# Two-layer trunk on one core: gate projections moved into their own heads, value tiles behind the next block's projections, boundary transpositions spread

## The chip, the cores and the metric

The kernel runs on one core of a Trainium2 chip. TensorE multiplies matrices, VectorE (DVE), ScalarE (ACT) and GpSimd (POOL) work element by element, and SyncE (SP) issues most transfers (DMAs). The metric is the device time of one execution in microseconds (us); lower is better.

## The reference

Two layers over x of 1 x 1024 x 1024, in fp32; after each a layer norm of alpha * x + layer(x).

```python
def _even_layer(x, ...):
    a_x, a_g, b_q, b_k, b_v, b_g = split(x @ w_in)         # six projections of width 1024
    a_h = _rg_lru(_causal_dwconv(a_x, conv_w, conv_b), ...)  # 8 blocks: gates, then h = a * h + u
    y_a = a_h * silu(a_g)
    # 8 heads: w = exp(log_sigmoid(z) + sum of log_sigmoid(-z) over later keys), strictly causal
    y_b = _stick_breaking(b_q, b_k, b_v) * silu(b_g)
    return concat(y_a, y_b) @ w_out
def _odd_layer(x, ...):
    q, k, v, g = split(x @ w_in)                            # 16 query heads, 2 key/value heads of 64
    o = _swa_sinks_alibi(q, k, v, sinks)                    # window of 128
    return (o * silu(g)) @ w_out
```

## The kernel before

The whole program is one function, `trunk`. Each fp32 operand is kept as a high and a low part, and a product is three matmuls (`mm3`, L110 to L112): high by high, high by low, low by high, mostly on tiles of 128x512. The low part of a result comes from PSUM with a copy on ScalarE and a subtraction on VectorE (`split_psum`, L118 and L119). Weights come in by `load_piece`: a DMA, then two GpSimd operations for the high and the low part (L102, L103). The framework decides the order on each engine from the order of the code, the dependencies and the free buffers.

The work runs in stages. First, eight recurrent blocks: `lru_main(f)` makes the gates of block f, a scan (L492) and a gated output, and stashes it in DRAM. Its own TensorE work is small, so a queue of generators, `Filler` (L34), is pumped between its steps: it takes so much work, by a rate in rough us, and always from the generator that stands first. In the queue are the value tiles (`v_tiles`, table VT: one or two tiles of 8 products x 3 for each block), and the projections of the next block (`lru_proj(f + 1)`: ax and ag, 48 products each). At f == 2 the weights of the second half of the values are loaded (`load_wv(1, d)`): the raw tiles go into buffers of the tags qh and ql, ScalarE casts them (L219), VectorE makes the low part.

Second, eight attention heads (`attn_all`), twelve units each: score z (L313 to L315), mask on the diagonal (L317), two sigmoids (L320, L321), scan (L329), product (L331, B), and, two units later, transpositions of B (L339), eviction (wt), and the products with v (L355 to L362). Between units the filler is pumped with the next head's projections: k, q and g, 48 products each, as `head_proj(n + 1)`. In the last head the filler is `early_out`: 72 products of the output projection into three PSUM tiles (opeX0 to opeX2). They need `prep(0)` to `prep(7)`: two DMAs, casts on ScalarE (L519), a subtraction on VectorE (opwh) and one on GpSimd (opwl), both L521.

Third, the rest of the output projection (`even_products`: the fourth tile opeX3 first, then opeZ; `prep` runs ahead by nine), the loads of x (xpre), and the layer norm, whose scaling runs on GpSimd (L636) and whose last addition runs on VectorE (L641). `x1_transposes(t)` transposes two rows of blocks at a time (L708) into the operands of the next layer. Then the boundary: half 1 of the odd layer's projections ok, ov and oq0, with `x1_transposes(0)` and `(1)` between, then half 0, the attention in windows, and the last output projection.

Of the kernel before, what the change touches and what calls it, by code (L numbers as in the profile page):

```python
# [52 lines left out]
def trunk(ctx, tc, x, xT_in, w_even, w_even_v, w_even_out, w_gate, lru_vec,  # L53
# [113 lines left out]
    def proj_ftile(src, ft, name, evac, halves=(0, 1), eng="pool"):  # L167
        get = w_ftile(src, ft, name, eng)
        for hf in halves:
            yield from proj_half(get, hf, name, evac)  # L170

    ytile = {}
    fill = Filler()
# [18 lines left out]
    def evac_qk(which, n):  # L192
        def f(hf, ps):
            h = wt_(which + "h", f"{which}h{n}_{hf}")
            l = wt_(which + "l", f"{which}l{n}_{hf}")
            split_psum(ps, h, l)
            qk[which, n, hf] = (h, l)
        return f

    def evac_gate(key):  # L200
        def f(hf, ps):
            if hf == 0:
                ytile[key] = slot(f"y{key[0]}{key[1]}", F32)
            y = ytile[key][:, hf, :]
            nc.scalar.activation(y, ps, AF.Sigmoid)
            nc.vector.tensor_tensor(out=y, in0=ps, in1=y, op=ALU.mult)
        return f
# [39 lines left out]
    def head_proj(n):  # L247
        yield from proj_ftile(w_even, 8 + n, f"k{n}", evac_qk("k", n), (1, 0))
        yield from proj_ftile(w_even, n, f"q{n}", evac_qk("q", n), (1, 0))
        yield from proj_ftile(w_even, 16 + n, f"g{n}", evac_gate(("b", n)))  # L250

    def stash(kind, t, tile_):
# [21 lines left out]
    def load_ya(n):  # L274
        ya_in[n] = slot(f"yain{n}", F32)
        for i, kind in enumerate(("A21", "S3")):
            nc.sync.dma_start(ya_in[n][:, i, :], yst[kind, n])
# [16 lines left out]
    rate = [0.0]  # L294

    def attn_all():
# [77 lines left out]
        for idx in range(len(units) + LAG + 1):  # L374
            while vpend:
                v_stage(*vpend.pop(0))
            if idx < len(units):
                n, i, g = units[idx]
                if (i, g) == (NS - 2, 1):
                    w_sums(n)  # L380
                if (i, g) == (NS - 1, 1):
                    fill.drain()
                    load_ya(n)
                    if n + 1 < SB_HEADS:
                        load_v(n + 1)
                        fill.add(head_proj(n + 1))
                        rate[0] = 31.2 / 12
                    else:
                        for t in range(8):
                            prep(t)  # L390
                        fill.add(early_out())
                        rate[0] = 16.4 / 12
                u_stage(n, i, g)
                pend.append(units[idx])
            if idx >= LAG and pend:
                n, i, g = pend.pop(0)
                t_stage(n, i, g)
                if i % 2 == 0 and g == 0:
                    vpend.append((n, i // 2))
            yield  # L400
# [106 lines left out]
    def prep(k):  # L507

        if k >= 8 * len(PRODUCTS):
            return  # L510
        i, t = divmod(k, 8)
        yop, w_op, _ = PRODUCTS[i]
        res = []
        for tag, src in (("wh", yst[yop, t]),
                         ("wl", yst[w_op, t] if isinstance(w_op, str) else w_even_out[w_op[0], w_op[1] + t])):
            raw = wpool.tile([P, HALF], F32, tag=tag, name=f"raw{tag}{k}", bufs=5)
            nc.sync.dma_start(raw, src)
            hl = slot(f"op{tag}{k}", F32R)
            nc.scalar.copy(hl[:, 0, :], raw)  # L519
            eng = nc.vector if tag == "wh" else nc.gpsimd  # L520
            eng.tensor_tensor(out=hl[:, 1, :], in0=raw, in1=hl[:, 0, :].bitcast(F32), op=ALU.subtract)  # L521
            res.append(hl)
        ops[k] = res
# [10 lines left out]
        f(b, y[:, 1, c], w[:, 0, :], start=False, stop=t == 7)  # L534

    def early_out():
        for p in range(3):
            op[0, p] = bank(XB[p], f"opeX{p}")
        for t in range(8):
            for p in range(3):  # L540
                step_mm(t, p)
                yield C_512
# [17 lines left out]
    for f in range(8):  # L560
        q, sts = VT[f]
        if f == 2:
            for d in range(ND):
                load_wv(1, d)
        fill.add(v_tiles(q, sts))
        if f + 1 < 8:
            fill.add(lru_proj(f + 1))
        else:
            load_v(0)
            fill.add(head_proj(0))  # L570
        r = (5.2 * len(sts) + (20.8 if f < 7 else 31.2)) / 4
        for _ in lru_main(f):
            fill.pump(r)
        fill.drain()
# [202 lines left out]
    with ExitStack() as dctx:  # L777
# [176 lines left out]
                pass  # L954

        gk = w_ftile(w_odd, 8, "ok", pool=slots)
        run(proj_half(gk, 1, "ok", evac_k))
        x1_transposes(0)
        xth.update(x1h)
        xtl.update(x1l)  # L960
        gv = w_ftile(w_odd, 9, "ov", pool=slots)
        run(proj_half(gv, 1, "ov", evac_v))
        x1_transposes(1)
        gq = w_ftile(w_odd, 0, "oq0")
        run(proj_half(gq, 1, "oq0", evac_q(0)))
        v_transposes(1)
        run(proj_half(gk, 0, "ok", evac_k))
        run(proj_half(gv, 0, "ov", evac_v))
# [76 lines left out]
```

## Time and profile before

| | |
|---|---|
| time, median of 3 runs | 1261.37 us (1260.93 to 1263.18) |
| the profiled execution's own time | 1261.14 us |
| its span in the profile | 1259.4 us |
| mean granted TensorE clock | 0.994 |
| busy: TensorE / VectorE / ScalarE / GpSimd | 98% / 68% / 50% / 50% |
| HBM traffic | 100.70 MB read, 37.75 MB written |

The span is what the profiler covers; all times of the trace count from its start. Busy shares are means over stages that have different limits. The profiler models the ends of matmuls, which are pipelined, so an end can lie later than the start of the next one. The granted clock is a share of TensorE's full speed.

### The profile page before, as it was taken

How to read it: one execution, taken by the hardware profiler on the slowest of the kernel's cores; microseconds unless marked ns; L12 is line 12 of the kernel's file. 1: busy time of each engine (PE TensorE's matmuls, PEld its weight loads, DVE VectorE, ACT ScalarE, POOL GpSimd, SP SyncE). 2: the span in 40 equal slices, each digit the busy share in tenths (PEclk: the TensorE clock that was granted, in tenths of full speed). 3: DMA queues.
4: the chain of work that ended last, by engine and by line, in shares of the span. 5: the costliest groups of instructions: out<-in, count | busy, mean ns of one | idle time of the engine just before them, and what ended most of it. 6: DMA issues, size and time to landing. Idle time of an engine off the chain costs nothing.

```text
span 1259.4 us, 18456 instructions
## 1 busy us (share of the span) xinstructions
PE 1228.9 (98%) x6176; PEld 1038.1 (82%) x6176; DVE 855.7 (68%) x1705; ACT 623.5 (50%) x1291; POOL 631.1 (50%) x720
## 2 busy tenths in 40 slices
PE   8999999999999999999999899999999999999997
PEld 6888788888888888888887778887888888887886
DVE  7354756556556767667668859587367877788367
ACT  5255546646333434434335447444277777778300
POOL 3334435435625454554445369666455555555440
PEclk9999999999999999999999999999999999999999
DMA  7312422234414254352457299700211101111022
GB/s 256 130 50 76 147 96 80 80 117 143 144 58 150 87 167 134 116 168 74 153 183 227 96 334 313 237 33 27 65 34 35 34 27 34 35 34 60 18 83 101
DMA packets 87791, 139.67 MB, mean 111 GB/s; under 512 B 10000, under 2 KB 27792, under 8 KB 87440
## 3 DMA queue, kind: packets, MB, share of 16 engines
q1 hardware_dynamic: 87696, 138.49, 33.2%
q8 instruction: 49, 0.80, 0.3%
q14 instruction: 46, 0.38, 0.1%
HBM read 100.70 MB, written 37.75 MB: 110 GB/s over the span
## 4 chain that ended last, share of the span: by engine, by line
PE 85%; DVE 6%; DMA 2%; ACT 2%; issue 2%; POOL 2%; POOLq 0%; SPq 0%; DVEq 0%; ACTq 0%
PE pjv L110 2%; PE pjv L111 2%; PE pjv L112 2%; PE pj_k L112 2%; PE pj_k L111 2%; PE pj_q L110 2%; PE pj_k L110 2%; PE pj_oq L110 2%; PE pj_q L112 2%; PE pj_oq L111 2%; PE pj_q L111 2%; PE pj_oq L112 2%; PE pj_og L110 2%; PE pj_g L110 2%; PE pj_og L111 2%; PE pj_g L112 2%
## 5 line engine op out<-in xcount | busy, mean ns | idle before, releaser
L521 POOL TENSOR_TENSOR opwl<-rawwl,opwl 128x512 fp32r<-128x512 f32 x56 | 88.8, 1611 | 36.1 <-ACT opwl L519 35.9
L320 ACT ACTIVATE C<-z 128x512 f32<-128x512 f32 (+3 forms) x96 | 47.4, 494 | 112.8 <-DVE z L317 85.5
L889 POOL TENSOR_SCALAR S<-S,sm 128x256 f32<-128x256 f32 (+1 forms) x128 | 59.8, 482 | 73.0 <-DVE sm L887 28.7
L884 ACT ACTIVATE S<-S,sm 128x256 f32<-128x256 f32 (+1 forms) x128 | 62.5, 490 | 53.6 <-DVE sm L880 51.9
L521 DVE TENSOR_TENSOR opwh<-rawwh,opwh 128x512 fp32r<-128x512 f32 x56 | 72.4, 1326 | 20.2 <-ACT opwh L519 20.1
L331 DVE TENSOR_TENSOR B<-B,C 128x512 f32<-128x512 f32 (+3 forms) x96 | 72.2, 752 | 10.1 <-DVE C L329 0.5
L329 DVE TENSOR_TENSOR_SCAN C<-C,one 128x512 f32<-128x512 f32 (+1 forms) x64 | 60.7, 949 | 16.7 <-ACT C L320 16.6
L118 ACT CAST wt<-tr 128x512 fp32r<-128x512 f32 (+3 forms) x96 | 46.6, 486 | 27.9 <-PE tr L339 27.4
L119 DVE TENSOR_TENSOR wt<-tr,wt 128x512 fp32r<-128x512 f32 (+3 forms) x96 | 52.5, 547 | 7.2 <-ACT wt L118 6.9
L110 PE MATMUL pjv<-wv,xh 128*128 128x512 f32 x128 | 49.9, 401 | 7.7 <-ACT wv L219 7.7
L329 DVE TENSOR_TENSOR_SCAN C<-C,C,one 128x512 f32<-128x512 f32 x32 | 42.0, 1313 | 18.3 <-ACT C L320 18.2
L519 ACT CAST opwh<-rawwh 128x512 fp32r<-128x512 f32 x56 | 34.8, 621 | 36.9 <-DMA rawwh<-stS 15.5
L110 PE MATMUL pj_k<-xh,wh_k 128*128 128x512 f32 x128 | 52.3, 408 | 0.0
L532 PE MATMUL opeX<-opwl,opwh 128*128 128x512 f32 x128 | 51.0, 402 | 1.0 <-DVE pvt L367 1.0
L110 PE MATMUL pj_q<-xh,wh_q 128*128 128x512 f32 x128 | 51.9, 405 | 0.0
L110 PE MATMUL pj_og<-x1h,wh_og 128*128 128x512 f32 x128 | 51.9, 405 | 0.0
L110 PE MATMUL pj_g<-xh,wh_g 128*128 128x512 f32 x128 | 51.8, 405 | 0.0
L110 PE MATMUL pj_oq<-x1h,wh_oq 128*128 128x512 f32 x128 | 51.8, 404 | 0.0
L112 PE MATMUL pj_k<-xh,wl_k 128*128 128x512 f32 x128 | 51.7, 404 | 0.0
L534 PE MATMUL opeX<-opwl,opwh 128*128 128x512 f32 x128 | 51.5, 403 | 0.0
L533 PE MATMUL opeX<-opwl,opwh 128*128 128x512 f32 x128 | 51.5, 403 | 0.0
L339 PE MATMUL tr<-ident,B 128*128 128x128 f32 x288 | 47.3, 273 | 4.2 <-DVE B L331 4.1
(314 smaller groups left out, 4333.3 us busy)
## 6 DMA issues: line engine op xcount, KB each, us to landing
vst<-vhl SPq DMA_DIRECT2D x16, 512.0 KB, 3.2
rawwh<-stS SPq DMA_DIRECT2D x32, 256.0 KB, 4.1
rawwl<-stT SPq DMA_DIRECT2D x32, 256.0 KB, 4.1
rawwh<-stA SPq DMA_DIRECT2D x24, 256.0 KB, 3.9
rawwl<-in_w_even_out_dram SPq DMA_DIRECT2D x24, 256.0 KB, 3.7
xraw<-in_xT_dram SPq DMA_DIRECT2D x16, 256.0 KB, 5.4
wvraw<-in_w_even_v_dram SPq DMA_DIRECT2D x16, 256.0 KB, 4.3
wr_ax<-in_w_even_dram SPq DMA_DIRECT2D x16, 256.0 KB, 2.9
```

The lines of the kernel that those rows point to most:

```text
L110: nc.tensor.matmul(ps, wh, xh, start=start, stop=False)
L111: nc.tensor.matmul(ps, wh, xl, start=False, stop=False)
L112: nc.tensor.matmul(ps, wl, xh, start=False, stop=stop)
L119: nc.vector.tensor_tensor(out=l, in0=ps, in1=h.bitcast(F32), op=ALU.subtract)
L329: nc.vector.tensor_tensor_scan(cr, cr, one.broadcast_to([P, W]), init, ALU.mult, ALU.mult)
L331: nc.vector.tensor_tensor(out=B[:, :W], in0=B[:, :W], in1=C[:, 1:W + 1], op=ALU.mult)
L521: eng.tensor_tensor(out=hl[:, 1, :], in0=raw, in1=hl[:, 0, :].bitcast(F32), op=ALU.subtract)
L532: f(b, y[:, 0, c], w[:, 0, :], start=fresh, stop=False)
L533: f(b, y[:, 0, c], w[:, 1, :], start=False, stop=False)
L534: f(b, y[:, 1, c], w[:, 0, :], start=False, stop=t == 7)
L884: nc.scalar.activation(Sb[:, j, lo:], Sb[:, j, lo:], AF.Exp, bias=nm[:, j:j + 1], accum_out=den[:, j:j + 1])
L889: nc.gpsimd.tensor_scalar(out=Sb[:, j, lo:], in0=Sb[:, j, lo:], scalar1=rec[:, j:j + 1], scalar2=0.0, op0=ALU.mult, op1=ALU.add)
```

## The change

The gate projection of an attention head leaves `head_proj` and becomes `gate_proj(n)`. It is queued at the start of head n itself, ahead of the next head's k and q. The fill of block 7 thus holds k and q of head 0 alone. In the last head the filler is its gate projection and then `early_out`, at a rate of 26 instead of 16.4 over twelve units, and the eight preparations are issued inside `early_out`, when the filler reaches it. In the recurrent stage the next block's projections are queued ahead of the value tiles. At the boundary the weights of ok, ov and oq0 are all loaded first, ok and ov are projected ahead of `x1_transposes(0)`, and oq0 between it and `x1_transposes(1)`.

```diff
--- before.py
+++ after.py
@@ -247,6 +247,8 @@
     def head_proj(n):
         yield from proj_ftile(w_even, 8 + n, f"k{n}", evac_qk("k", n), (1, 0))
         yield from proj_ftile(w_even, n, f"q{n}", evac_qk("q", n), (1, 0))
+
+    def gate_proj(n):
         yield from proj_ftile(w_even, 16 + n, f"g{n}", evac_gate(("b", n)))
 
     def stash(kind, t, tile_):
@@ -381,15 +383,14 @@
                 if (i, g) == (NS - 1, 1):
                     fill.drain()
                     load_ya(n)
+                    fill.add(gate_proj(n))
                     if n + 1 < SB_HEADS:
                         load_v(n + 1)
                         fill.add(head_proj(n + 1))
                         rate[0] = 31.2 / 12
                     else:
-                        for t in range(8):
-                            prep(t)
                         fill.add(early_out())
-                        rate[0] = 16.4 / 12
+                        rate[0] = 26.0 / 12
                 u_stage(n, i, g)
                 pend.append(units[idx])
             if idx >= LAG and pend:
@@ -534,6 +535,8 @@
         f(b, y[:, 1, c], w[:, 0, :], start=False, stop=t == 7)
 
     def early_out():
+        for t in range(8):
+            prep(t)
         for p in range(3):
             op[0, p] = bank(XB[p], f"opeX{p}")
         for t in range(8):
@@ -562,13 +565,13 @@
         if f == 2:
             for d in range(ND):
                 load_wv(1, d)
-        fill.add(v_tiles(q, sts))
         if f + 1 < 8:
-            fill.add(lru_proj(f + 1))
+            fill.add(lru_proj(f + 1), v_tiles(q, sts))
         else:
+            fill.add(v_tiles(q, sts))
             load_v(0)
             fill.add(head_proj(0))
-        r = (5.2 * len(sts) + (20.8 if f < 7 else 31.2)) / 4
+        r = (5.2 * len(sts) + 20.8) / 4
         for _ in lru_main(f):
             fill.pump(r)
         fill.drain()
@@ -954,15 +957,15 @@
                 pass
 
         gk = w_ftile(w_odd, 8, "ok", pool=slots)
+        gv = w_ftile(w_odd, 9, "ov", pool=slots)
+        gq = w_ftile(w_odd, 0, "oq0")
         run(proj_half(gk, 1, "ok", evac_k))
+        run(proj_half(gv, 1, "ov", evac_v))
         x1_transposes(0)
+        run(proj_half(gq, 1, "oq0", evac_q(0)))
+        x1_transposes(1)
         xth.update(x1h)
         xtl.update(x1l)
-        gv = w_ftile(w_odd, 9, "ov", pool=slots)
-        run(proj_half(gv, 1, "ov", evac_v))
-        x1_transposes(1)
-        gq = w_ftile(w_odd, 0, "oq0")
-        run(proj_half(gq, 1, "oq0", evac_q(0)))
         v_transposes(1)
         run(proj_half(gk, 0, "ok", evac_k))
         run(proj_half(gv, 0, "ov", evac_v))
```

Names in the rows below end in the block, head or piece and a number of the buffer. In the changed kernel lines from L250 on have numbers that are one to three higher.

ScalarE during recurrent block 2: ri2 are the block's gates, wv1d the casts of the second half's value weights, vhl the evictions of value tiles, xc3 the start of block 3. Before:

```order
L472 ACTIVATE ri2_0_0_1123<-g2_0_0_1119,vec_107 128x512
L472 ACTIVATE ri2_0_1_1129<-g2_0_1_1125,vec_107 128x512
L219 CAST wv10_1075<-wvraw10_1073 128x512
L219 CAST wv11_1080<-wvraw11_1078 128x512
L472 ACTIVATE ri2_1_0_1183<-g2_1_0_1179,vec_107 128x512
L472 ACTIVATE ri2_1_1_1189<-g2_1_1_1185,vec_107 128x512
L219 CAST wv12_1085<-wvraw12_1083 128x512
L219 CAST wv13_1090<-wvraw13_1088 128x512
```

And with the change:

```order
L118 CAST vhl06_1040<-pjv0_6_999 128x512
L473 ACTIVATE ri2_0_0_1123<-g2_0_0_1119,vec_107 128x512
L473 ACTIVATE ri2_0_1_1129<-g2_0_1_1125,vec_107 128x512
L219 CAST wv10_1075<-wvraw10_1073 128x512
L219 CAST wv11_1080<-wvraw11_1078 128x512
L219 CAST wv12_1085<-wvraw12_1083 128x512
L219 CAST wv13_1090<-wvraw13_1088 128x512
L219 CAST wv14_1095<-wvraw14_1093 128x512
L219 CAST wv15_1100<-wvraw15_1098 128x512
L118 CAST vhl07_1069<-pjv0_7_1044 128x512
L219 CAST wv16_1105<-wvraw16_1103 128x512
L436 ACTIVATE xc3_0_1168<-pj_ax3_0_1143,vec_107 128x512
```

The casts keep their place behind block 2's first gates; with the change evictions of the first half's value tiles and the eviction of block 3's projection stand among them.

TensorE at the last head's first score (z7_7_1; L313 to L315, and L315 to L317 with the change): opeX are the early products, pj_g7 the last head's gate projection. Before:

```order
L532 MATMUL opeX1_6674<-opwl2_6602,opwh2_6597 128x512
L533 MATMUL opeX1_6674<-opwl2_6602,opwh2_6597 128x512
L534 MATMUL opeX1_6674<-opwl2_6602,opwh2_6597 128x512
L313 MATMUL z7_7_1_6655<-kh7_1_6105,qh7_1_6267 128x512
L314 MATMUL z7_7_1_6655<-kl7_1_6106,qh7_1_6267 128x512
L315 MATMUL z7_7_1_6655<-kh7_1_6105,ql7_1_6268 128x512
L532 MATMUL opeX2_6675<-opwl2_6602,opwh2_6597 128x512
L533 MATMUL opeX2_6675<-opwl2_6602,opwh2_6597 128x512
L534 MATMUL opeX2_6675<-opwl2_6602,opwh2_6597 128x512
```

And with the change:

```order
L360 MATMUL pv6_2_6419<-wt6_5_0_6333,vl6_5393 128x256
L341 MATMUL tr6_2_0_6482<-ident_67,B6_2_0_6392 128x128 x3
L112 MATMUL pj_g7_0_6538<-xh01_131,wl_g7_0_6529 128x512
L315 MATMUL z7_7_1_6508<-kh7_1_6197,qh7_1_6351 128x512
L316 MATMUL z7_7_1_6508<-kl7_1_6198,qh7_1_6351 128x512
L317 MATMUL z7_7_1_6508<-kh7_1_6197,ql7_1_6352 128x512
L110 MATMUL pj_g7_0_6538<-xh01_131,wh_g7_0_6528 128x512
L111 MATMUL pj_g7_0_6538<-xl01_132,wh_g7_0_6528 128x512
L112 MATMUL pj_g7_0_6538<-xh01_131,wl_g7_0_6529 128x512
```

Early products stood ahead of that score; now gate products stand on both sides of it, and the early products follow later.

TensorE at the boundary: x1tr0 and x1tr1 are the transpositions of the first two groups (L708, and L711 with the change), pj_ok, pj_ov and pj_oq0 the odd projections, half 1 or 0. Before:

```order
L112 MATMUL pj_ok_1_8422<-x1h13_8261,whl_ok_1_8419 128x512
L708 MATMUL x1tr0_1_8470<-ident_67,xpre_7091 128x128
L708 MATMUL x1tr0_2_8477<-ident_67,xpre_7091 128x128 x3
L708 MATMUL x1tr0_3_8484<-ident_67,xpre_7091 128x128 x4
L708 MATMUL x1tr1_0_8528<-ident_67,xpre_7091 128x128
L708 MATMUL x1tr1_1_8535<-ident_67,xpre_7091 128x128
L708 MATMUL x1tr1_2_8542<-ident_67,xpre_7091 128x128
L708 MATMUL x1tr1_0_8528<-ident_67,xpre_7091 128x128 x3
L708 MATMUL x1tr1_1_8535<-ident_67,xpre_7091 128x128 x3
L708 MATMUL x1tr1_2_8542<-ident_67,xpre_7091 128x128 x3
L708 MATMUL x1tr1_3_8549<-ident_67,xpre_7091 128x128 x4
```

And with the change:

```order
L111 MATMUL pj_oq0_1_8540<-x1l13_8262,wh_oq0_1_8440 128x512
L112 MATMUL pj_oq0_1_8540<-x1h13_8261,wl_oq0_1_8441 128x512
L711 MATMUL x1tr1_0_8571<-ident_67,xpre_7091 128x128 x4
L711 MATMUL x1tr1_1_8578<-ident_67,xpre_7091 128x128 x4
L711 MATMUL x1tr1_2_8585<-ident_67,xpre_7091 128x128 x4
L711 MATMUL x1tr1_3_8592<-ident_67,xpre_7091 128x128 x4
L110 MATMUL pj_ok_0_8608<-x1h00_8504,whl_ok_0_8414 128x512
L110 MATMUL pj_ov_0_8641<-x1h00_8504,whl_ov_0_8424 128x512
L110 MATMUL pj_oq0_0_8668<-x1h00_8504,wh_oq0_0_8434 128x512
```

The two groups stood in one piece ahead of the value projection; now the second group follows half 1 of oq0, and half 0 of all three projections starts behind it.

## Rows read from the trace of the kernel before

**Rows 1.** The page, part 1: busy us, share of the span, instructions, by engine.

```profile
PE 1228.9 (98%) x6176; PEld 1038.1 (82%) x6176; DVE 855.7 (68%) x1705; ACT 623.5 (50%) x1291; POOL 631.1 (50%) x720
```

**Rows 2.** Windows; the first row names the columns.

```profile
core 0: us, PE busy (x) PEld busy (x) DVE busy (x) ACT busy (x) POOL busy (x), PEclk, DMA share, GB/s
150.00:325.00 175.00, 175.00 (x773) 144.93 (x772) 100.98 (x135) 92.27 (x118) 83.04 (x78) 1.00 0.32 106
132.60:136.00 3.40, 3.40 (x10) 2.66 (x9) 1.53 (x4) 2.12 (x4) 1.29 (x1) 0.50 1.04 389
578.20:628.40 50.20, 50.20 (x274) 43.13 (x273) 34.97 (x63) 19.66 (x47) 25.13 (x31) 1.00 0.40 131
628.40:687.00 58.60, 55.59 (x289) 47.11 (x288) 46.12 (x72) 27.83 (x63) 27.69 (x31) 0.97 0.60 197
687.00:726.10 39.10, 33.05 (x197) 27.70 (x195) 32.75 (x65) 18.16 (x46) 16.09 (x22) 1.00 0.35 123
726.50:729.90 3.40, 3.40 (x10) 2.62 (x9) 2.71 (x4) 3.40 (x7) 3.32 (x3) 0.50 0.46 120
```

**Rows 3.** Waits of TensorE from 125, 675 and 868 us: total us, times, longest.

```profile
PE pjv L110 <- ACT wv L219: 2.7, 1, 2.7
...
PE tr L339 <- DVE B L331: 4.1, 3, 3.0
...
PE x1tr L708 <- DVE xpre L641: 1.2, 1, 1.2
PE x1tr L708 <- DVE x1l L119: 0.8, 2, 0.5
PE pj_ov L110 <- POOL whl_ov L102: 0.8, 1, 0.8
```

**Rows 4.** Timeline, 125 to 132 us: start, us, engine, instruction, [idle before].

```profile
125.64 2.31 DVE L492 TENSOR_TENSOR_SCAN xc<-ri,xc,t 128x512 f32<-128x512 f32 x1
...
128.01 0.33 SPq L215 DMA_DIRECT2D wvraw<-in_w_even_v_dram  x1
...
131.27 1.14 ACT L219 CAST wv<-wvraw 128x512 fp32r<-128x512 f32 x2 [6.19 <-DMA wvraw<-in_w_even_v_dram]
```

**Rows 5.** Timeline around the last head, VectorE and TensorE.

```profile
628.36 0.40 PE L313 MATMUL z<-kh,qh 128*128 128x512 f32 x1
...
686.99 0.39 PE L313 MATMUL z<-kh,qh 128*128 128x512 f32 x1
...
717.36 0.27 DVE L317 TENSOR_TENSOR z<-z,mask 128x128 f32<-128x128 f32 x1
...
726.08 0.47 PE L532 MATMUL opeX<-opwl,opwh 128*128 128x512 f32 x1 [1.03 <-DVE pvt L367]
```

**Rows 6.** Tiles on VectorE, 660-727 and 330-630 us: ns min/median/max, starts.

```profile
L521 DVE TENSOR_TENSOR opwh<-rawwh,opwh x9: 677/958/1773, 667.4 to 726.0; 128x512 fp32r<-128x512 f32 x9
...
L119 DVE TENSOR_TENSOR kl<-pj_k,kh x12: 672/676/685, 336.4 to 595.4; 128x512 fp32r<-128x512 f32 x12
```

**Rows 7.** Chain of waits, 727 to 750 us: start, us, what.

```profile
729.22 5.82 DMA stS<-s
...
735.06 5.37 DMA xpre<-in_x_dram
...
740.49 5.35 DMA rawwh<-stS
...
745.91 0.62 ACT opwh L519
...
748.58 0.50 PE opeZ L533
```

**Rows 8.** Timeline of GpSimd, 864 to 873 us.

```profile
864.47 2.17 POOL L102 TENSOR_SCALAR whl_ok<-wr_ok 128x512 fp32r<-128x512 f32 x2
866.60 2.55 POOL L103 TENSOR_TENSOR whl_ok<-wr_ok,whl_ok 128x512 fp32r<-128x512 f32 x2
869.27 2.41 POOL L636 TENSOR_TENSOR xpre<-xpre,gb 128x1024 f32<-128x1024 f32 x1
```

**Rows 9.** Waits of ScalarE over the span: total us, times, longest.

```profile
ACT qh L118 <- PE z L314: 24.2, 7, 3.5
```

## The prediction

> **What bounds the kernel now.** I read the page first: TensorE is busy for 1228.9 of 1259.4 us [rows 1]. So time is won only where TensorE waits, or where it is granted less than its full clock. Then I read windows of 25 to 60 us, and in each compared TensorE's time with the number of its products. The undisturbed stretch sets the price: 773 products in 175.00 us at a granted clock of 1.00, 0.227 us for a 128x512 product [rows 2]. An attention head without trouble, from 578.2 to 628.4 us, takes 50.2 us, in which 144 products of filler (three projections of 48) are 32.7 us; 17.5 us are left for the head itself. The longest lists of waits of TensorE, taken in the stretches that the diff touches, then show three places [rows 3]: one wait of 2.7 us near 132 us, waits around the last head, and waits at the boundary between the layers. The rest of the program keeps its order, so I cost these three, and the head boundaries between, where the filler's order changes.
>
> The profiled execution took 1261.14 us, its span 1259.4; it lies 0.2 us under the median of 1261.37, so the sum is made against 1261.14 and needs no shift.
>
> **Value tiles behind the next block's projections.** Before, the first value tile of the second half (pjv1_0) waits 2.7 us for the cast of its weights [rows 3]. The chain behind it: the raw weights go into a buffer that the running block still uses; its scan starts at 125.64 and takes 2.31, the DMA is issued at 128.01, and the cast begins at 131.27, after an idle of 6.19 on ScalarE that the DMA ended [rows 4]. Behind the wait TensorE runs ten products in 3.40 us at a granted clock of 0.50, the lower of its two levels (1.2 of 2.4 GHz); at half the clock half of that stretch, 1.7 us, is lost (some of the ten rows lie only partly in it) [rows 2]. Together 4.4 to 4.5.
> The change leaves the DMAs and casts behind the same block's chain, but puts the next block's 96 projection products ahead of the value tile. By the two orders, 216 products stand between the second gate product of the block (which feeds the scan) and pjv1_0, where 153 stood: 63 products, 14.3 us more cover for a wait of 2.7. The chain can be late by a further 11.6 before TensorE stops. Bounds: 0 gain, if the casts were pushed back as far, and 4.5. I take 4.5, since the casts keep their place between the same block's activations. What is late next is the next block's gate: its projections come earlier, which helps it.
>
> **Gate projection inside its own head.** The 48 gate products (10.9 us) are only moved. Block 7 carries 48 fewer, heads 0 to 6 carry 144 as before (this head's gate, the next head's k and q), and the last head 120 (gate and 72 early output products) where it had 72.
> Up to the last head everything comes 10.9 us earlier. Head 6 began at 628.36 [rows 5], so it begins at 617.5, and head 7, one period of 50.2 later [rows 2], at 667.7 (before: 686.99 [rows 5], since part of the 72 early products already stood ahead of it). From there to the first product of the fourth output tile (opeX3, 726.08 before [rows 5]) TensorE has 17.5 + 10.9 + 72 x 0.227 = 44.7 us of work: 712.4 if it never waits, a gain of 13.7. That is the ceiling, and it is exactly what heads 6 and 7 lose now: the stretch before the score has 58.60 - 55.59 = 3.0 us idle with a clock of 0.97, the one after it 39.10 - 33.05 = 6.0 [rows 2].
> The 3.0 us are the wait for B in the middle [rows 3]: the eight preparations (an opwh subtraction on VectorE each) fall into the stretch in which VectorE is already at 46.12 of 58.60, and TensorE has nothing to run while it waits. Now the gate products lie there as cover. The 6.0 us stand mostly in the tail: from the mask of the last score but one at 717.36 to opeX3 at 726.08 [rows 5] the chain score, sigmoid, scan, transposition, product runs with little beside it. The gate comes first in the filler and is used up by then, so this tail stays; I keep the whole 6.0. Then opeX3 starts at 712.4 + 6.0 = 718.4, a gain of 7.7.
> Can VectorE keep up? A steady head has 34.97 us of it [rows 2]; the last head loses four low parts of k and q at 0.676 and takes up eight preparations at the median of 0.958 [rows 6]: 34.97 - 2.7 + 7.7 = 40.0, under 44.7. At the longest row, 1.773 [rows 6], it is 46.5, over it; a rival below.
> The same rows of the preparation run from 677 to 1773 ns for one form [rows 6]. The Trainium skill, "GPSIMD Engine Reference", section 8 "Key points", says that GpSimd shares its SBUF interfaces with VectorE and contends with VectorE instructions that have two SBUF inputs; this subtraction has two, and GpSimd makes the other low part at the same time. By that rule the preparations inside the last head would sit at the long end, and the time would be the 1252.4 of the first rival.
> Behind opeX3 nothing is won or lost: the 13th prepared pair hangs on the last stash, a DMA from 729.22, the load of x at 735.06, the raw operand issued at 740.49 and ScalarE's cast at 745.91, and the product that needs it is at 748.58, 22.5 us behind opeX3 [rows 7]. That chain starts with the last head's output, so it moves with it. The 3.40 us at clock 0.50 behind opeX3 [rows 2] lie under it; if they vanish, TensorE waits there instead.
> Bounds: 13.7 above; below 0, if the preparations cost what the gate covers. I take 7.7.
>
> **Boundary.** Before, all x1tr transpositions of the first two groups stand together; TensorE waits 1.2 + 0.8 in them and 0.8 for the value projection's weights [rows 3], 2.8; each wait hides some 0.2 us more, since a recorded transposition end lies later than the next could start: 3.5. With the change 48 products (10.9 us) of ov and oq0 lie between the transpositions. The weights must be there: GpSimd runs its two high parts from 864.47 (2.17), two low parts (2.55), then a scaling of 2.41 [rows 8]. With ov's and oq0's pieces ahead by the new order, ov's first low part comes at about 871 and the second near 877; TensorE wants them near 875 and 879. The scalings that the later transpositions need end near 880 and 881.5 with VectorE's addition; TensorE comes there near 886. Behind them the first product of ok's other half now waits some 0.5 us for an eviction that two q evictions precede. So 3.5 - 0.5 = 3.0, bounds 0 (weights late by what was won) and 3.5.
>
> **Sum.** 4.5 + 7.7 + 3.0 = 15.2; 1261.14 - 15.2 = 1245.9, so 1246.
>
> **The rivals.**
> *VectorE and GpSimd collide in the last head.* Eight preparations at 1.773 instead of 0.958 put 6.5 us more on VectorE [rows 6], of which the chain of the units waits behind nearly all: the head's term falls to 1.2, the time to 1252.4. For it: the spread of that row. Against it: the median, and the gate's cover. 0.13.
> *The last head reaches its floor.* If gate products are left over for the tail, the 6.0 idle us go too: the term is 13.7, the time 1240. Against it: the filler is taken in order and at a rate that empties it by then. 0.07.
> *The weights at the boundary come late*, by the 2 to 4 us of margin: its term is 0, the time 1249. For it: GpSimd has no free place between 864 and 880. 0.05.
> *The loads behind the last head don't move with it.* If the 13th pair is set by DMAs and not by the head's end, the 7.7 are given back as a wait at opeZ, the time 1253.6. Against it: the chain of waits starts at the stash [rows 7]. 0.03.
> *Slower: the first score of each head waits for its q.* With the gate first, q's last two halves end each head's filler; half 1, which the first score reads, ends only 24 products, 5.4 us, ahead of it. Its eviction takes 0.62 (a cast of that size [rows 7]) and 0.676 [rows 6], and must wait until the old q tile's last score is done: 24.2 us in 7 times now, at most 3.5 [rows 9]. 3.5 + 1.3 = 4.8 fits into 5.4. If the wait grows past 4.1, each head pays the excess seven times: at 2.2 us each the 15.2 are gone, and at the 3.5 of the row's longest the time is 1246 + 24.5 = 1270. 0.08, of which 0.05 for more than 2.5 us a head.
> My forecast has the remaining 0.64.
>
> **How the numbers follow.** The three terms' own bounds give 1242 to 1250 for the forecast. The range takes in the floor of the last head (1240) and the collision (1252.4): 1240 to 1253; left out are the loads (0.03), q (0.08) and half of the floor case, about 0.15. A measurement of this kernel can tell some 0.2%, 2.5 us, from no change. Faster by more is every case but q: 0.92. Within it: q at 1.8 to 2.5 us a head, 0.03. Slower: q above that, 0.05.
>
> **What would show it.** The wait of pjv for wv and its stretch at clock 0.50 gone; the first score of head 0 some 15 us earlier (10.9 and 4.5), that of head 7 at 686.99 - 23.8 = 663.2; opeX3 at 726.08 - 12.2 = 713.9, with no wait of 3 us for B but with idle time in the tail; opeZ's 13th pair still 22.5 us behind; waits at x1tr and pj_ov under 1 us together. It is wrong if head periods grow past 50.2 with waits of z for qh, if opwh's subtraction is near 1.7 us each in the last head, or if pj_ov waits for whl_ov longer than now.

## The result, and the profile after

The changed kernel is slower: 1269.86 us (median of 4, 1268.68 to 1273.86) against 1261.15 (median of 4), a ratio of 1.0071 with a 95% interval of 1.0046 to 1.0096. The forecast was 1246, with a range of 1240 to 1253. Its profiled execution took 1269.25 us, its span 1267.5.

Where the time went is read first from landmarks, the first product of each stage. Two of them in the kernel before, from the timeline of TensorE (the first score of head 0, and the first score of the window attention; the others stand in [rows 5] and [rows 7]):

```profile
327.49 0.39 PE L313 MATMUL z<-kh,qh 128*128 128x512 f32 x1
...
915.11 0.22 PE L871 MATMUL s<-KH,QA 128*128 128x128 f32 x1
```

The same view of the changed kernel: first score of head 0, first score of head 7, opeX3, the product that needs the 13th prepared pair, and the first score of the window attention.

```profile
325.99 0.39 PE L315 MATMUL z<-kh,qh 128*128 128x512 f32 x1
...
677.08 0.39 PE L315 MATMUL z<-kh,qh 128*128 128x512 f32 x1
...
734.38 0.47 PE L533 MATMUL opeX<-opwl,opwh 128*128 128x512 f32 x1 [1.02 <-DVE pvt L369]
...
757.17 0.50 PE L534 MATMUL opeZ<-opwl,opwh 128*128 128x512 f32 x1 [0.17 <-POOL opwl L522]
...
923.24 0.22 PE L874 MATMUL s<-KH,QA 128*128 128x128 f32 x1
```

| landmark | before | after | shift | forecast |
|---|---|---|---|---|
| first score of head 0 | 327.49 | 325.99 | -1.5 | -15.4 |
| opeX3 | 726.08 | 734.38 | +8.3 | -12.2 |
| product with the 13th pair | 748.58 | 757.17 | +8.6 | -12.2 |
| first score of the window attention | 915.11 | 923.24 | +8.1 | -15.2 |
| span | 1259.4 | 1267.5 | +8.1 | -15.2 |

So 13.9 us of the error stand ahead of the first head, 6.6 between there and opeX3, 2.5 at the boundary, and at most 0.3 elsewhere. Each of the three terms missed. In three kernels further below that leave the recurrent stage as it was, the first landmark stands at 326.60 to 327.14, so a landmark of one trace is good to about a microsecond. The waits of TensorE over the whole span name the three places (the second row is the start of the program; together with the wait of [rows 3] it is one row of 7.7 in the kernel before):

```profile
PE pjv L110 <- DVE vhl L119: 10.7, 4, 3.2
PE pjv L110 <- ACT wv L219: 4.7, 1, 4.7
PE tr L341 <- DVE wt L119: 2.8, 2, 2.5
PE pj_oq L110 <- DVE QB L838: 2.1, 1, 2.1
```

**The recurrent stage.** The wait for wv near 132 us is gone, as forecast. In its place TensorE waits four times for the eviction of a value tile (vhl). The timeline around the first shows the chain, in order of time: the last product of tile 4, ScalarE's copy, VectorE busy with the block's scans and gated outputs and then its share of the eviction, and TensorE's first product of tile 5.

```profile
79.58 0.39 PE L112 MATMUL pjv<-wv,xl 128*128 128x512 f32 x1
...
81.05 0.58 ACT L118 CAST vhl<-pjv 128x512 fp32r<-128x512 f32 x1
...
81.79 1.65 DVE L493 TENSOR_TENSOR_SCAN xc<-ri,t 128x512 f32<-128x512 f32 x1
83.47 1.60 DVE L496 TENSOR_TENSOR gg<-xc,gg 128x512 f32<-128x512 f32 x1
84.99 1.27 DVE L493 TENSOR_TENSOR_SCAN xc<-ri,xc,t 128x512 f32<-128x512 f32 x1
86.30 0.69 DVE L496 TENSOR_TENSOR gg<-xc,gg 128x512 f32<-128x512 f32 x1
87.02 0.69 DVE L499 TENSOR_TENSOR s<-gg,gg 128x512 f32<-128x512 f32 x1
87.63 0.68 DVE L119 TENSOR_TENSOR vhl<-pjv,vhl 128x512 fp32r<-128x512 f32 x1
...
88.37 0.51 PE L110 MATMUL pjv<-wv,xh 128*128 128x512 f32 x1 [2.50 <-DVE vhl L119]
```

Tile 4 is complete at 80, and its bank comes free at 88.3, because VectorE works in order and five instructions of the scan's chain stand ahead of the eviction. The next tile must go into the same bank: the tag pv has one. The same tile in the kernel before, in the same view:

```profile
57.43 0.39 PE L112 MATMUL pjv<-wv,xl 128*128 128x512 f32 x1
57.85 0.59 ACT L118 CAST vhl<-pjv 128x512 fp32r<-128x512 f32 x1 [4.75 <-PE pjv L112]
58.47 0.69 DVE L119 TENSOR_TENSOR vhl<-pjv,vhl 128x512 fp32r<-128x512 f32 x1 [6.10 <-ACT vhl L118]
...
63.55 0.39 PE L110 MATMUL pjv<-wv,xh 128*128 128x512 f32 x1
```

There the tile ended ahead of the scan's chain, VectorE was idle, and the bank was free at 59.2, 1.7 us after the last product began, where it now takes 8.7. Other work lay between the two tiles, up to 63.55. So the move has two effects on one bank: its eviction falls behind the scan's chain, and what could run meanwhile has already run. Which of the two would have been enough alone no run here tells.

The windows show what else was lost and what was not: behind the wait at 126.57 (127.7 to 131.1 us) the granted clock is 0.53, behind the one at 88.37 it is 1.00; the heads run at their old period, and the last head lasts 57.3 us:

```profile
88.50:91.90 3.40, 3.40 (x15) 2.79 (x16) 0.00 (x0) 0.00 (x0) 0.00 (x0) 1.00 0.60 237
127.70:131.10 3.40, 3.40 (x10) 2.69 (x9) 1.38 (x2) 1.10 (x2) 0.00 (x0) 0.53 0.98 328
185.00:200.00 15.00, 12.50 (x49) 9.94 (x48) 10.83 (x10) 5.43 (x8) 6.76 (x6) 0.89 0.34 122
626.90:677.10 50.20, 50.20 (x274) 43.09 (x273) 34.85 (x63) 19.73 (x47) 19.76 (x25) 1.00 0.45 148
677.10:734.40 57.30, 50.53 (x260) 41.07 (x258) 47.30 (x76) 27.88 (x65) 29.83 (x31) 0.94 0.49 165
```

Two of the four waits (the second, and the third at 196.29) are followed by the lower clock: 3.40 x (1 - 0.53) = 1.6 us, and 15.0 x (1 - 0.89) = 1.6. With 10.7 of waits that is 13.9 us lost, less the 4.5 that the old wait cost: 9.4. The landmark says the same, 10.9 - 1.5 = 9.4.

**The last head.** VectorE is busy for 47.30 of 57.30 us, where 40.0 were forecast. Tiles of opwh on VectorE from 676 to 735 us (ns min/median/max), and the timeline of VectorE and TensorE there, with one GpSimd instruction:

```profile
L522 DVE TENSOR_TENSOR opwh<-rawwh,opwh x9: 659/1712/1779, 693.1 to 734.3; 128x512 fp32r<-128x512 f32 x9
```

```profile
688.83 1.28 DVE L331 TENSOR_TENSOR_SCAN C<-C,C,one 128x512 f32<-128x512 f32 x1 [0.91 <-ACT C L322]
...
696.67 4.60 DVE L522 TENSOR_TENSOR opwh<-rawwh,opwh 128x512 fp32r<-128x512 f32 x3
701.19 2.31 DVE L331 TENSOR_TENSOR_SCAN C<-C,C,one 128x512 f32<-128x512 f32 x1
...
704.55 1.72 POOL L269 TENSOR_TENSOR wq7a<-wq7b,wq7a 128x512 f32<-128x512 f32 x1
...
705.06 0.68 DVE L119 TENSOR_TENSOR wt<-tr,wt 128x512 fp32r<-128x512 f32 x1
...
718.92 1.11 PE L341 MATMUL tr<-ident,B 128*128 128x128 f32 x4 [2.49 <-DVE wt L119]
```

The median of the subtraction is 1.71 us where it was 0.958 [rows 6], and a scan of the same form takes 2.31 where it took 1.28 twelve microseconds earlier. Not every instruction is longer: the subtraction that makes a wt has one operand in PSUM, and it keeps its 0.68 us beside a GpSimd instruction (704.55 to 706.27). Where VectorE's time goes is read from windows of one kind of instruction (us, busy, count, granted clock): the eight opwh subtractions in the kernel before and in the changed one, then the twelve scans of a head, in head 6 and in the last head of the changed kernel.

```profile
628.40:687.00 58.60, 9.19 (x8) 0.97 0.60 197
...
677.10:734.20 57.10, 11.14 (x8) 0.94 0.49 166
...
626.90:677.10 50.20, 12.12 (x12) 1.00 0.45 148
677.10:734.40 57.30, 15.45 (x12) 0.94 0.49 165
```

VectorE is late, the filler is used up, and TensorE waits 2.49 us for a wt. With that wait the granted clock falls:

```profile
718.90:724.90 6.00, 5.98 (x16) 4.88 (x17) 3.08 (x6) 1.35 (x3) 0.10 (x1) 0.50 0.55 173
```

In the row of the last head TensorE is idle for 57.30 - 50.53 = 6.8 us, near the 6.0 of the forecast, but busy for 50.53 where 44.7 were forecast; 57.30 x (1 - 0.94) = 3.4 of the difference is the clock.

**The boundary.** The waits of the last three rows of [rows 3] are gone; one of 2.1 us has taken their place. VectorE and TensorE there:

```profile
897.07 1.36 DVE L799 CAST distb<-dist 128x256 bf16<-128x256 f32 x1 [0.66 <-POOL dist L797]
898.47 0.68 DVE L836 SCALAR_TENSOR_TENSOR QA<-pj_oq,QA 64x512 fp32r<-64x512 f32 x1
899.16 0.69 DVE L838 SCALAR_TENSOR_TENSOR QB<-pj_oq,QB 64x512 fp32r<-64x512 f32 x1
...
900.00 0.47 PE L110 MATMUL pj_oq<-x1h,wh_oq 128*128 128x512 f32 x1 [2.10 <-DVE QB L838]
```

The eviction of oq0's half 1 frees the PSUM bank into which its half 0 must go, and ahead of it on VectorE stands a cast of the window attention's constants, which first waits 0.66 us for GpSimd and then lasts 1.36 (0.29 in the kernel before).

### The profile page after: what moved, and what is told of

The parts are those of the page before. It is cut to its first block, busy times and chain, and to the rows that moved or that the text cites. A ratio compares the mean times of both kernels' runs of the same rounds, so it can differ in the third digit from the quotient of the medians.

```text
span 1267.5 us, 18452 instructions
## 1 busy us (share of the span) xinstructions
PE 1231.5 (97%) x6176; PEld 1038.8 (82%) x6176; DVE 874.4 (69%) x1705; ACT 626.5 (49%) x1292; POOL 632.3 (50%) x720
## 4 chain that ended last, share of the span: by engine, by line
PE 77%; DVE 10%; issue 4%; ACT 3%; POOL 3%; DMA 3%; POOLq 0%; SPq 0%; ACTq 0%; DVEq 0%
PE pj_g L112 2%; PE pj_g L111 2%; PE tr L341 2%; PE pj_g L110 2%; PE pj_q L110 2%; PE pj_q L112 2%; PE pj_q L111 2%; PE pj_k L112 2%; PE pj_k L110 2%; PE pj_k L111 2%; PE opo L111 2%; PE opo L110 2%; PE opo L112 2%; PE pj_og L110 2%; PE pj_og L111 2%
## 5 line engine op out<-in xcount | busy, mean ns | idle before, releaser
L331 DVE TENSOR_TENSOR_SCAN C<-C,one 128x512 f32<-128x512 f32 (+1 forms) x64 | 60.0, 937 | 22.6 <-ACT C L322 22.5
L110 PE MATMUL pjv<-wv,xh 128*128 128x512 f32 x128 | 51.2, 411 | 15.4 <-DVE vhl L119 10.7
L370 POOL TENSOR_TENSOR yb<-pvt,yb 128x128 f32<-128x128 f32 x32 | 15.2, 476 | 78.4 <-DVE pvt L369 78.4
L520 ACT CAST opwh<-rawwh 128x512 fp32r<-128x512 f32 x56 | 34.8, 622 | 37.4 <-DMA rawwh<-stS 15.4
L534 PE MATMUL opeX<-opwl,opwh 128*128 128x512 f32 x128 | 51.9, 405 | 0.6 <-POOL opwl L522 0.5
L112 PE MATMUL pj_g<-xh,wl_g 128*128 128x512 f32 x128 | 51.9, 405 | 0.0
L111 PE MATMUL pjv<-wv,xh 128*128 128x512 f32 x128 | 51.6, 403 | 0.0
L535 PE MATMUL opeX<-opwl,opwh 128*128 128x512 f32 x128 | 51.5, 402 | 0.1
```

The lines of the kernel that those rows point to most:

```text
L110: nc.tensor.matmul(ps, wh, xh, start=start, stop=False)
L111: nc.tensor.matmul(ps, wh, xl, start=False, stop=False)
L112: nc.tensor.matmul(ps, wl, xh, start=False, stop=stop)
L331: nc.vector.tensor_tensor_scan(cr, cr, one.broadcast_to([P, W]), init, ALU.mult, ALU.mult)
L534: f(b, y[:, 0, c], w[:, 1, :], start=False, stop=False)
```

## The experiments

Theory: three separate losses, each where VectorE stands between TensorE and a PSUM bank or a tile: the value tiles' single bank, the collision of VectorE and GpSimd in the last head, and the constants ahead of oq0's eviction. The rivals stand with each run.

**Each part alone.** Three kernels make one part of the change each, with the lines of that part in the diff of the change and nothing else.

```diff
+            fill.add(lru_proj(f + 1), v_tiles(q, sts))     # values_alone: this order, for f < 7
...
+                    fill.add(gate_proj(n))                 # gate_alone: with gate_proj split off, both rates,
+                        fill.add(early_out())              # and the preparations inside early_out
...
+        run(proj_half(gv, 1, "ov", evac_v))                # boundary_alone: the last hunk
         x1_transposes(0)
+        run(proj_half(gq, 1, "oq0", evac_q(0)))
+        x1_transposes(1)
```

values_alone: 

> The kernel before with the value tiles queued behind the next block's projections, nothing else of the change. Theory (the value tiles share one PSUM bank, and with nothing queued behind them TensorE stops until VectorE has evicted the tile before): waits of pjv for vhl of 2.5 to 3.2 us, three or four of them, with stretches at half the clock, the wait for wv near 132 us gone; the recurrent stage 9.4 us longer by the trace of the whole change, less what comes of block 7's shorter fill, so 1268 to 1271 us. Rival (the four waits come of block 7's shorter fill or of the rates, not of the order in the queue): at most one such wait, and 1256 to 1259 us, the gain of 4.5 that was forecast.

Measured: 1273.91 us, ratio 1.0102 (1.0086 to 1.0117). The four waits for vhl are there, 10.7 us in all and 3.2 at most as in the whole change, and the first score of head 0 moves from 327.49 to 336.97, by 9.5. In the recurrent stage place and size of the loss are the theory's: the order in the queue does it by itself. The time is 3 us beyond the theory's bounds: the span is 11.9 us longer, so 2.4 are lost behind that landmark. There the granted clock is 0.54 for 6.80 us from 724.5 and 0.56 for 3.40 us from 758.7, some 4.6 us lost, where the kernel before has one stretch of 3.40 at 0.50 [rows 2]; why it falls oftener here is not shown.

gate_alone: 

> The kernel before with the gate projection inside its own head and the preparations inside the last head's filler, nothing else. Theory (VectorE and GpSimd collide there): the opwh subtraction at a median near 1.7 us in the last head, a wait of a transposition of 2 to 3 us there, 1.1 us gained: 1259 to 1261 us. Rival (the last head suffers from what came before it, not from the collision): the forecast gain of 7.7, so 1253 to 1255 us.

Measured: 1259.54 us, ratio 0.9988 (0.9978 to 0.9997), a gain of 1.9. The tile's row reads as in the whole change:

```profile
L522 DVE TENSOR_TENSOR opwh<-rawwh,opwh x9: 664/1710/1779, 684.4 to 724.6; 128x512 fp32r<-128x512 f32 x9
```

So the last head's trouble is not inherited from the recurrent stage.

boundary_alone: 

> The kernel before with the new boundary alone. Theory (one wait has taken the place of three: the first oq0 product of half 0 waits about 2 us for the eviction of half 1 that frees its PSUM bank): 0.4 us gained, 1260 to 1261.5 us, and no wait for whl_ov. Rival (the wait came from the shifted start of the stage): 3 us gained, 1257.5 to 1259 us.

Measured: 1262.60 us, ratio 1.0010 (1.0001 to 1.0020). The wait of pj_oq for QB is 2.1 us, that for whl_ov is gone. The time lies 1 us above the theory's bounds and far from the rival's: the new boundary is worth nothing. Here the wait, which ends at 891.13, is followed by the lower clock, 3.40 x (1 - 0.52) = 1.6 us more; in the whole change it is not (1.00 from 900 to 910 us):

```profile
892.50:895.90 3.40, 3.40 (x9) 2.62 (x9) 1.00 (x2) 0.00 (x0) 0.00 (x0) 0.52 0.02 5
```

**The value tiles' bank.** Two kernels hold the whole change and give the value tiles a second bank, first by turns, then by place.

```diff
-            ps = bank("pv", f"pjv{q}_{st}")
+            ps = bank(("pv", "z")[st % 2], f"pjv{q}_{st}")                     # two_banks
+            ps = bank("z" if (q, st) == (1, 7) or st != sts[-1] else "pv", ...)  # banks_by_place
```

two_banks: 

> The whole change with every second value tile in a PSUM bank of the tag z in place of pv. Theory (one bank for all value tiles): the waits of pjv for vhl fall from 10.7 us in four to under 1 us, and with the half-clock stretches 13 to 14 us come back: 1255 to 1257.5 us. Rival (the eviction that stands behind the block's scan on VectorE is what stops TensorE, whatever the bank, or the gates now wait for the bank): waits of 8 us and more stay, at pjv or at g: 1266 to 1270 us.

Measured: 1258.10 us, ratio to the kernel before 0.9977 (0.9967 to 0.9986): 11.8 us better than the whole change by the medians, where 13 to 14 were expected. The waits of pjv for vhl fall from 10.7 to 0.7, but the gates, which use the tag z, now wait once for a value tile's eviction:

```profile
PE g L110 <- DVE vhl L119: 1.7, 1, 1.7
...
PE pjv L110 <- DVE vhl L119: 0.7, 1, 0.7
```

banks_by_place: 

> The whole change with the value tiles' PSUM banks chosen by place: the first of a pair and the last tile of all in a bank of the tag z, the last of each block in pv. Theory (a bank whose tile is evicted behind the block's scan must not be the one that TensorE needs next): no wait of pjv or g for vhl over 0.5 us, the 1.87 at g and 0.85 at pjv of the version with alternate banks and the half-clock stretch behind them come back, 3 to 4 us: 1254 to 1255.5 us. Rival (any bank of tag z makes the gates wait): a wait of g of 1.5 us and more, 1257 to 1259 us.

Measured: 1257.00 us (1255.56 to 1259.90), ratio 0.9961 (0.9948 to 0.9974). The wait at g is gone, as the theory said; 0.7 at pjv stays, and a wait of pj_ag for xc of 1.2 us is new. The time is at the lower bound of the rival, whose mechanism, a wait of g, is not there; the theory promised 1.5 us too much. It counted on a stretch at half the clock behind the wait at g, and two_banks has none there (1.00 from 115 to 150 us). The first score of head 0 comes at 313.72, 13.8 us before the old one: 10.9 of moved work and 2.9 of the 4.5 forecast for the value tiles.

**The last head.** Two kernels, both with the gate part alone, take the eight opwl subtractions away from GpSimd.

```diff
-            eng = nc.vector if tag == "wh" else nc.gpsimd
+            eng = nc.vector if tag == "wh" or k < 8 else nc.gpsimd   # gate_low_on_dve
...
+            if tag == "wl" and k < 8:
+                nc.scalar.copy(hl[:, 1, :], raw)                     # gate_low_left_out
+            else:
+                eng.tensor_tensor(...)                               # as before
```

gate_low_on_dve: 

> The gate part alone, with the low parts of the first eight weight operands (opwl) also on VectorE in place of GpSimd, so that VectorE has 16 subtractions where it had 8. Theory (VectorE's subtraction lasts 1.7 us only because GpSimd works at the same time): each of the 16 near 0.7 us, VectorE's busy time in the last head falls from 47.8 to 44 to 46 us though it has more instructions, opeX3 1 to 4 us earlier than with the gate part alone: 1255.5 to 1258.5 us. Rival (VectorE simply has too much to do in the last head): 8 more subtractions add 5 to 14 us of VectorE there, opeX3 later: 1263 to 1270 us.

Measured: 1253.06 us, ratio 0.9927 (0.9912 to 0.9942), better than the theory's bounds. VectorE has eight instructions more, and the median of each row is at its short end; a few instructions still take 1.78. From the same kernel, the two tiles on VectorE:

```profile
L522 DVE TENSOR_TENSOR opwh<-rawwh,opwh x13: 660/679/1780, 683.0 to 723.2; 128x512 fp32r<-128x512 f32 x13
...
L522 DVE TENSOR_TENSOR opwl<-rawwl,opwl x8: 675/680/1780, 683.6 to 702.7; 128x512 fp32r<-128x512 f32 x8
```

gate_low_left_out: 

> The gate part alone; the subtraction that makes the low part of the first eight weight operands is left out, and ScalarE writes a second copy of the operand in its place, so GpSimd has eight instructions less in the last head and VectorE as many as before. Theory (collision): the median of opwh falls from 1.71 us to 0.7 to 1.0 (GpSimd's weight sums still collide with some), VectorE's busy time in the last head falls by 4 to 7 us, opeX3 4 to 7 us earlier: 1252.5 to 1256 us. Rival (the place of the preparations in VectorE's order): opwh may be shorter, but the waits of the transpositions stay and the time is within 1 us of the gate part alone, 1258.5 to 1260.5 us.

Measured: 1252.40 us, ratio 0.9923 (0.9909 to 0.9938): at the theory's lower bound, though a copy on ScalarE was added for each subtraction left out. The last head from its first score to opeX3, by windows: with the gate part alone,

```profile
668.40:724.70 56.30, 49.36 (x260) 40.21 (x258) 47.46 (x76) 27.70 (x65) 29.81 (x31) 0.97 0.50 168
```

with the low parts on VectorE,

```profile
667.00:718.30 51.30, 47.42 (x260) 39.22 (x258) 45.03 (x84) 27.93 (x65) 17.48 (x23) 1.00 0.53 185
```

and with them left out:

```profile
668.00:717.10 49.10, 46.42 (x259) 39.40 (x258) 38.86 (x76) 31.41 (x73) 17.18 (x23) 1.00 0.54 193
```

The reader is to see the VectorE column: 84 instructions in 45.03 us where 76 took 47.46, and 38.86 when GpSimd does nothing in their place. What VectorE's work costs here depends on what GpSimd does beside it. By the Trainium skill, "SBUF — State Buffer", section "Who interferes with whom", the two share one pair of ports, which one of them holds for a whole instruction. The trace agrees that a subtraction of 0.66 us takes 1.7 beside a GpSimd subtraction; whether the pair is held or shared no run here tells.

before_low_on_dve: the same line alone in the kernel before. 

> The kernel before with the first eight opwl on VectorE and nothing of the change. Theory (the mend helps because the preparations now lie inside the last head, where gate products cover VectorE; before, eight more subtractions fall on the end of head 6, where VectorE is already busiest): within 2.5 us of the kernel before, 1259 to 1264 us. Rival (the collision alone costs the last head its time, with or without the gate): 6 us and more gained, 1253 to 1256 us.

Measured: 1258.85 us, ratio 0.9976 (0.9967 to 0.9986), a gain of 2.5, just past the theory's bound and 2.9 us short of the rival's. The low parts alone gain 2.5 us, the gate part alone 1.9, both together 9.4, so by the medians five come only of the two together. By the spans of the profiled executions the three are 3.7, 1.0 and 7.2, and 2.5 come of the two together: both counts say that the two help each other; by how much is open.

**The boundary.** The constants are made behind the projections.

```diff
-        swa_consts()
...
         v_transposes(0)
+        swa_consts()
         for _ in swa_all():
```

boundary_consts: 

> The boundary part alone, with the constants of the window attention (swa_consts, three GpSimd operations and a VectorE cast that waits for them) called behind the projections in place of ahead of them. Theory (that cast, 1.36 us long after an idle of 0.67 on VectorE, stands ahead of the eviction that frees oq0's bank): the wait of oq0 falls from 2.1 to under 0.5 us, 2 us less than the boundary part alone: 1258.5 to 1260.5 us. Rival (the eviction is late by its own chain, two copies and two VectorE operations): the wait stays over 1.2 us and the time within 0.7 us of the boundary part alone.

Measured: 1260.10 us (1257.91 to 1261.37), ratio 0.9982 (0.9972 to 0.9992), 2.5 us under the boundary part alone by the medians, 3.5 when each is taken against the kernel before in its own set of runs (2.3 faster and 1.2 slower); the wait gives back 1.9 and the clock behind it 1.6. The late constants without the new boundary were not run. The product that waited 2.1 us:

```profile
888.62 0.47 PE L110 MATMUL pj_oq<-x1h,wh_oq 128*128 128x512 f32 x1 [0.17 <-DVE QB L835]
```

**All together.** all_mended is the whole change with banks by place, the first eight opwl on VectorE and the late constants.

> The whole change with its three mends: value tiles' banks by place, the first eight opwl on VectorE, the window attention's constants behind the projections. Theory (the three losses are separate, and the parts add): the recurrent stage 2.9 us shorter than in the kernel before by its trace (the mended value tiles), 9.4 from the gate part with opwl on VectorE, 2.3 from the boundary with late constants: 14.6 in all, 1246 to 1249 us. Rival (the parts share a resource, so that a mend in one place is given back in another, at the 13th prepared pair or at the tail of the last head): 1250 to 1254 us.

Measured: 1248.86 us (1247.77 to 1250.83), ratio 0.9901 (0.9884 to 0.9918), the fastest version here, at the theory's upper bound and below the rival's range. The gain is 12.5 where the parts' sum was 14.6, so most of it adds; the missing 2 us are not accounted for. The largest waits of TensorE that are left (the first is the start of the program):

```profile
PE pjv L110 <- ACT wv L219: 4.9, 1, 4.9
PE opv L923 <- DVE ptl L119: 1.6, 2, 1.3
PE pv L358 <- DVE pvt L369: 1.2, 2, 0.9
PE opeX L534 <- DVE opwl L522: 1.1, 1, 1.1
```

mended_old_values goes back to the old order of the value tiles in one bank. 

> As all_mended, with the value tiles ahead of the next block's projections and in one bank, as in the kernel before. Theory (the moved value tiles are worth 2.9 us once they have their banks): 2 to 4 us slower than all_mended, 1248.5 to 1252 us, with the wait of pjv for wv near 132 us back. Rival (the recurrent stage's gain is given back later): within 1 us of all_mended.

Measured: 1251.66 us, ratio 0.9920 (0.9905 to 0.9935), 2.8 us slower than all_mended, as in the theory, and the wait near 132 us is back (pjv waits for wv 7.3 us in two, in place of 4.9 in one).

all_mended_rate20 changes `rate[0] = 26.0 / 12` to `20.0 / 12`. 

> As all_mended, with the last head's filler at a rate of 20 in place of 26 over its twelve units, so that early products are left for the end of the head. Theory (the tail of the last head waits 5 us because no filler is left): the waits of pv and tr in the tail fall by 2 to 4 us, 1243 to 1246 us. Rival (what is left over stands behind the tail's chain, so the tail waits as before and the products come on top): 1247 to 1251 us.

Measured: 1249.37 us, ratio 0.9907 (0.9892 to 0.9922): no gain, and my theory of the tail falls; the time is the rival's. The waits of pv and tr are 2.3 us in all_mended already, not 5, and fall to 1.5; waits for an opwl in opeX and opeZ rise from 1.5 to 4.3. opeX3 comes at 716.28 in place of 716.69, a difference of 0.4 that the time doesn't show.

## Why the prediction was wrong, step by step

- **Value tiles: forecast a gain of 4.5, measured a loss of 9.4.** The step that failed is "what is late next": I named the next block's gate, which is helped, and not the next value tile. I counted 63 products of cover for the weights and asked neither when VectorE evicts a value tile's bank nor what TensorE has to run meanwhile. Before, the eviction came ahead of the scan's chain and projections lay behind the tile; with the change it comes behind the chain, and the projections are done. My lower bound of 0 was therefore no bound, and none of the five rivals had this bank in it. values_alone shows the loss, the two kernels with a second bank show its cause. The gain forecast for the weights is real but smaller: 2.9 by the landmark of banks_by_place, 2.8 by the times of all_mended and mended_old_values. The first scores of these two lie only 0.8 us apart (314.40 and 315.24), but the second is ahead by 60 us already, in a part that is the same in both (238 products against 230, 1.8 us).
- **Last head: forecast 7.7, measured 10.9 + 398.6 - 408.4 = 1.1.** (From the first score of head 0 to opeX3 it was 398.6 us, and is 408.4 with 10.9 more work.) The step that failed is VectorE's load: 34.97 - 2.7 + 7.7 = 40.0 was forecast and 47.30 measured. Eight preparations were priced at the median of 0.958, from a place where GpSimd had less to do; they take 11.14 us in place of 7.7. The scans were left at a steady head's length; they take 15.45 in place of 12.12. Both could be read ahead of the run in the stretch from 628.4 to 687: there eight preparations take 9.19 us, 1.15 each, since a sum needs the mean and not the median, and the scans take 14.75. For TensorE the late VectorE costs a wait of 2.49 us and 3.4 us of clock, for which the sum had no term. The rival of the collision gave 1.2 for this term; its mechanism was right, and its chance of 0.13 was too low. That its price fits is partly luck: it put 6.5 us on eight subtractions, which cost 3.4, and the scans cost another 3.3. The rule of the Trainium skill that I weighed there, "GPSIMD Engine Reference", section 8, spoke against the change, and the trace bears it out with 1.71 against 0.68.

  With opwl off GpSimd the stretch from score to opeX3 takes 49.1 to 51.3 us, and the forecast was 50.7. This too is partly luck: gate_low_left_out has TensorE busy for 46.42 us and idle for 2.7, where the forecast had 44.7 and "the whole 6.0". The work was too small because the last head also holds the products of its last two units, which in other heads run behind the next head's first score: 147 products of its own where head 6 has 129. And the ceiling of 13.7 is not "exactly what heads 6 and 7 lose now": the rows named for it hold 3.0 + 6.0 us idle and 58.60 x (1 - 0.97) = 1.8 of clock, 10.8.
- **Boundary: forecast 3.0, measured 0.5 by the landmarks** (from the 13th pair to the window attention: 166.53 before, 166.07 after), and nothing that the time shows. Right: the old waits go. The step that failed is the wait that follows: I put 0.5 us at the first product of ok's half 0, which waits 0.15, and the wait stands at oq0's half 0, with 2.1. I didn't walk VectorE's row up to that product's eviction, where the constants' cast stands.
- **Right:** head 6 keeps its period, 50.20 us with 274 products, so the rival of q, the only one on the slower side, did not happen; the 13th pair is 22.8 us behind opeX3 (22.5 before), so that chain moves with the head's end; no wait for whl_ov.

The three misses, 13.9 + 6.6 + 2.5 = 23.0, are the distance of the span from its forecast, 8.1 + 15.2 = 23.3, within 0.3 us.

## What to carry to other kernels

Before work is moved to the end of a filler queue, list the PSUM bank that each of its pieces needs and what stands ahead of that bank's eviction on its in-order engine; filler that follows a piece is also the cover for that eviction. The duration of a VectorE instruction that reads SBUF alone is only good for a place where GpSimd does the same as in the row it was taken from, and a sum takes the mean of such a row, not its median; moving eight subtractions from GpSimd to VectorE made VectorE's total shorter. And a part that costs time is not for that reason a bad part: with three small mends the same change goes from 0.7% slower to 1.0% faster.

## What the runs showed of the hardware

- The same VectorE forms beside a busy GpSimd: the subtraction 1.7 us in place of 0.66, the scan of 128x512 2.31 in place of 1.28. A subtraction of the same size with one operand in PSUM (wt) keeps 0.68.
- Four waits of TensorE of 2.5 to 3.2 us in the recurrent stage have different consequences: behind the first (2.50 us at 88.37) the granted clock stays at 1.00, behind the second, equally long in the same kind of work, it is 0.53 for 3.4 us. The wait of 2.1 us for QB is followed by 1.00 in the whole change and by 0.52 for 3.40 us in boundary_alone. What tells them apart these runs don't show.
